# Rope scores as two float32r matmuls over stacked halves, and forgetting attention transposed by key block

## Chip, cores, metric

The kernel runs on one core of one Trainium2 chip. The metric is device time in microseconds (us) of one launch, less is better. Times are medians of a few executions; one further execution was taken with the hardware profiler, and all rows come from it.

## What is computed

Three transformer blocks follow one another on one sequence of 512 tokens with 1024 features, all in float32: block 1 (mLSTM beside differential attention, a feed-forward, a gated embedding), block 2 (a stick-breaking attention layer, then a latent attention layer) and block 3 (feed-forward, a hybrid of a spatial gating unit and a "forgetting" attention, feed-forward). Two pieces matter here.

Latent attention, 8 heads: each query and key has 128 "nope" features of its own and 64 "rope" features that are rotated by position; the rope key is shared by all heads before its norm.

```
k = concatenate([k_nope, k_pe], axis=-1)          # 128 + 64 features
q = rms_norm(q, q_head_norm); k = rms_norm(k, k_head_norm)
q = concatenate([q[..., :128], rope(q[..., 128:], pos)], axis=-1)
k = concatenate([k[..., :128], rope(k[..., 128:], pos)], axis=-1)
o = causal_softmax_attention(q, k, v, 1 / sqrt(192))
```

Forgetting attention, 8 heads of 64 features, in blocks of 128 queries:

```
logits = q_block @ k[:q1].T * scale + cum[q] - cum[k]    # cum: running sum of log forget gates
p = softmax(where(kpos <= qpos, logits, -1e30))
out_block = p @ v[:q1]
```

## The kernel before

Features lie on partitions and tokens on the free axis, so a tile is 128 features by 512 tokens. The large products with weights are made in three float32r matmuls for each 128 input features: weights and activations are split into a high part (rounded to float32r by a ScalarE copy) and a low part (VectorE subtracts the high part), and hi·hi, lo·hi and hi·lo are summed in PSUM (lines 429 to 431 for feature-major outputs, 439 to 441 for token-major ones; tiles `hi`, `lo`, `wh`, `wl`, output `pm`). The matmuls of attention take float32 operands as they are. In the rows a float32 matmul is two instructions, a float32r or bfloat16 one is one.

**Order.** The Python code is a program order; a list scheduler then places each instruction on its engine, and every engine runs its own list in order. The attention loops hide the latency of softmax in two ways: `self.fill()` takes the next piece from a list of projections that are not urgent, and `self.later(f, depth)` puts transposes and values of a finished block of queries into a queue, whose pieces are run some steps later. `flush()` empties that queue at the end and takes one filler after each piece.

**Latent attention** (`mla`) goes by 4 pairs of heads. For a pair, `kv`, `q`, `scales` and `keys` make its operands; for pairs 1 to 3 they are fillers in the loop of the pair before. `keys` broadcasts the 16 per-token key scales over partitions by matmuls with an identity: once for the shared rope key (line 1287, tile `pbc`, 8 matmuls of 64 output rows, product `krc` on line 1289), and once for each head's nope key (line 1292, tile `bc`). A score block is three matmuls into one PSUM bank (tile `mls`): the nope part over 128 rows (line 1326), the rope part over 64 rows, the upper or lower half of the partitions by head (line 1327), and the causal mask as bfloat16 (line 1328). Blocks are 128 queries by 512, 384, 256 and 128 keys.

**Forgetting attention** (`fox_pair`) also goes by 4 pairs of heads and 4 query blocks from the longest to the shortest. Scores (`fxs`, lines 1712 and 1714) of the two heads go to two PSUM banks of the role `sc`; softmax leaves a tile `fxp` for each head. One step later `apply` transposes the block's key blocks (line 947, tile `tr`, one PSUM bank of the role `tr` that both heads use in turn; ScalarE copies it to `aT` on line 949) and multiplies by the values (line 1701, tile `fxo`, 64 output rows for each head). The spatial gating unit is a filler here: its last projections run in the loop of pair 3, its norm's statistic and the first half of the output projection (`out_a`) behind them.

## Time and profile before

| | before |
|---|---|
| median of 3 executions | 2506.77 us (2504.44 to 2509.23) |
| the profiled execution | 2498.9 us |
| its span, first to last instruction | 2497.1 us |
| TensorE (PE) busy | 2438.4 us, 98% |
| VectorE (DVE), ScalarE (ACT), GpSimd (POOL) busy | 53%, 39%, 3% |
| mean granted TensorE clock | 0.988 of full speed |
| HBM traffic | 96 GB/s over the span |

A matmul's record runs from its start to its modelled end, and the next one starts before that end, so in a stream of matmuls the cost of one is the distance to the next start. The busy time of a group counts overlapped time once.

### The profile page before, as it was taken

The numbers are of one execution on the slowest core, as the hardware profiler recorded it, in microseconds if no ns is written. First come the engines' busy times: TensorE is split into PE (matmuls) and PEld (weight loads), VectorE is DVE, ScalarE is ACT, GpSimd is POOL, SyncE is SP. The second block draws the span as 40 slices with busy tenths as digits, with TensorE's granted clock in tenths as the row PEclk, the third lists the DMA queues.
The fourth block names the chain that finished last, engine by engine and source line by source line (L and its number), as shares of the span: only waits on it lengthen the run. The fifth ranks groups of instructions, "written<-read, shape, count | busy, mean of one in ns | idle before, by whom it ended". The sixth has DMA issues, their size and how long they took to land. (4 is left out here: it accounts for less than half of the span.)

```text
span 2497.1 us, 31348 instructions
## 1 busy us (share of the span) xinstructions
PE 2438.4 (98%) x12622; PEld 1994.1 (80%) x12622; DVE 1313.5 (53%) x2220; ACT 983.0 (39%) x1575; POOL 62.7 (3%) x62
## 2 busy tenths in 40 slices
PE   8999999999999999999999999999999999999998
PEld 6877788888888787777877798888898768888887
DVE  7536556774775664446555654223365465432333
ACT  5423433442444445655324533222245344322221
POOL 0000000000000000000000000000010001000001
PEclk9999999999999999999999999999999989999999
DMA  5223225433433332222322113233213101323321
GB/s 188 93 90 101 90 97 185 135 123 114 152 119 119 126 109 77 68 81 83 113 71 85 37 66 118 93 101 101 93 54 103 61 26 60 96 93 101 100 87 49
DMA packets 71746, 240.78 MB, mean 96 GB/s; under 512 B 8232, under 2 KB 11184, under 8 KB 71600
## 3 DMA queue, kind: packets, MB, share of 16 engines
q1 hardware_dynamic: 71600, 238.78, 29.1%
q8 instruction: 99, 1.62, 0.3%
q14 instruction: 47, 0.39, 0.0%
HBM read 236.64 MB, written 2.11 MB: 96 GB/s over the span
## 5 line engine op out<-in xcount | busy, mean ns | idle before, releaser
L429 PE MATMUL pm<-hi,wh 128*128 128x512 f32 (+1 forms) x2736 | 1045.1, 383 | 11.1 <-ACT hi L393 7.3
L430 PE MATMUL pm<-lo,wh 128*128 128x512 f32 (+1 forms) x2736 | 1042.8, 381 | 0.0
L431 PE MATMUL pm<-hi,wl 128*128 128x512 f32 (+1 forms) x2736 | 1040.7, 380 | 0.0
L419 ACT CAST wh<-raw 128x1024 fp32r<-128x1024 f32 (+1 forms) x372 | 382.3, 1029 | 827.0 <-PE pm L430 581.5
L420 DVE TENSOR_TENSOR wl<-raw,wh 128x1024 fp32r<-128x1024 f32 (+1 forms) x372 | 445.0, 1196 | 448.8 <-ACT wh L419 422.2
L429 PEld LDWEIGHTS pm<-hi,wh 128*128 128x128 f32 x2736 | 517.2, 189 | 110.9 <-ACT hi L393 8.9
L430 PEld LDWEIGHTS pm<-lo,wh 128*128 128x128 f32 x2736 | 517.0, 189 | 96.5 <-issue 3.8
L431 PEld LDWEIGHTS pm<-hi,wl 128*128 128x128 f32 x2736 | 516.8, 189 | 96.1 <-issue 3.6
L439 PE MATMUL pm<-wh,hi 128*128 128x256 f32 x400 | 116.0, 290 | 4.9 <-ACT vt L816 4.9
L1393 DVE CUSTOM_DVE_ANT_0 adaw<-adaw,cb 128x1024 f32<-128x1024 f32 x72 | 87.9, 1220 | 55.7 <-DMA adaw<-in_w_ada 55.5
L441 PE MATMUL pm<-wh,lo 128*128 128x256 f32 x400 | 115.1, 288 | 0.0
L440 PE MATMUL pm<-wl,hi 128*128 128x256 f32 x400 | 114.2, 286 | 0.0
L1472 DVE TENSOR_TENSOR sg<-sg,pm 128x512 f32<-128x512 f32 x44 | 30.2, 686 | 132.8 <-PE pm L431 132.7
L572 POOL TENSOR_TENSOR rc<-ms,nhalf 128x4 f32<-128x4 f32 (+2 forms) x29 | 38.6, 1333 | 2335.2 <-DVE ms L577 1779.3
L439 PEld LDWEIGHTS pm<-wh,hi 128*128 128x128 f32 x400 | 77.8, 194 | 5.8 <-ACT vt L816 5.3
L441 PEld LDWEIGHTS pm<-wh,lo 128*128 128x128 f32 x400 | 77.8, 194 | 0.5 <-issue 0.3
L440 PEld LDWEIGHTS pm<-wl,hi 128*128 128x128 f32 x400 | 77.8, 194 | 0.5 <-issue 0.2
L481 PE MATMUL pm<-hi,wh 128*128 128x256 f32 (+1 forms) x216 | 61.5, 309 | 9.9 <-ACT hi L400 7.1
L970 DVE SCALAR_TENSOR_TENSOR uy<-ur,vec,uy 128x511 f32<-128x511 f32 x88 | 65.7, 747 | 9.0 <-ACT uy L968 8.0
L258 DVE TENSOR_TENSOR acc<-acc,sq 128x512 f32<-128x512 f32 (+1 forms) x93 | 54.6, 595 | 24.0 <-ACT sq L254 22.8
L482 PE MATMUL pm<-lo,wh 128*128 128x256 f32 (+1 forms) x216 | 66.0, 307 | 0.3 <-DVE lo L1424 0.3
L483 PE MATMUL pm<-hi,wl 128*128 128x256 f32 (+1 forms) x216 | 66.2, 308 | 0.0
(350 smaller groups left out, 2363.7 us busy)
## 6 DMA issues: line engine op xcount, KB each, us to landing
raw<-in_w_gu SPq DMA_DIRECT2D x88, 512.0 KB, 3.3
adaw<-in_w_ada SPq DMA_DIRECT2D x72, 512.0 KB, 3.3
raw<-in_w_dn SPq DMA_DIRECT2D x48, 512.0 KB, 3.3
raw<-in_w_up SPq DMA_DIRECT2D x44, 512.0 KB, 3.3
raw<-in_w_g SPq DMA_DIRECT2D x16, 512.0 KB, 3.3
raw<-in_w_l0qk SPq DMA_DIRECT2D x16, 512.0 KB, 3.4
raw<-in_w_l SPq DMA_DIRECT2D x12, 512.0 KB, 3.3
X<-in_x SPq DMA_DIRECT2D x16, 256.0 KB, 5.6
```

The costliest lines, as they stand in the source:

```text
L419: nc.scalar.copy(wh[:, :n], raw[:, :n])
L420: nc.vector.tensor_tensor(wl[:, :n], raw[:, :n], wh[:, :n].bitcast(F32), ALU.subtract)
L429: self.nc.tensor.matmul(out, a, xh, start=start and k == 0, stop=False)
L430: self.nc.tensor.matmul(out, a, xl, start=False, stop=False)
L431: self.pe = self.nc.tensor.matmul(out, b, xh, start=False, stop=stop and k == n - 1)
L439: self.nc.tensor.matmul(out, xh[:, sl], a, start=start and k == 0, stop=False)
L440: self.nc.tensor.matmul(out, xh[:, sl], b, start=False, stop=False)
L441: self.pe = self.nc.tensor.matmul(out, xl[:, sl], a, start=False, stop=stop and k == len(x) - 1)
L482: self.nc.tensor.matmul(o[:, sl], wh[:, k], xl[:, sl], start=False, stop=False)
L483: self.nc.tensor.matmul(o[:, sl], wl[:, k], xh[:, sl], start=False, stop=k == 7)
L970: nc.vector.scalar_tensor_tensor(y[:, sh:], raw[:, :S - sh], self.v("fconv_w", 44 * (2 - sh) + f), y[:, sh:], mult, add)
L1393: nc.vector.tensor_tensor_reduce(w, w, cb, 0.5, 0.0, ALU.mult, ALU.add, mod[:, i:i + 1])
```

## The change

In latent attention the rope query of each head becomes one tile `qs` of 128 rows: its high part in 64 rows and its low part in the other 64. The rope key is scaled for each head apart (the same broadcast `bc` that scales the nope key), and split into two float32r tiles of 128 rows (both halves hold the shared key), kept in buffers of the weight pools (`krs`). Scores then take two float32r matmuls over 128 rows, with the key's high and its low part. The eight `pbc` matmuls of a pair are gone.

In forgetting attention the probabilities of a pair of heads stay in five tiles until all four query blocks are done. Then, in the next pair's loop, they are transposed by key block: five groups of four blocks, each filling one PSUM bank, in banks of the roles `tr` and `ms` in turn, and a last piece `values` multiplies each key block once by all its queries (512, 384, 256 and 128 columns).

```diff
-                r["qr"] = self.rope(r["q"].pop(0), self.v("qh_r"), cos, sin)
+                qr = self.rope(r["q"].pop(0), self.v("qh_r"), cos, sin)
+                r["qr"] = []
+                for own, other in (ROWS, ROWS[::-1]):
+                    y = self.t(F32R, "qs")
+                    nc.scalar.copy(y[own], qr[own])
+                    nc.vector.tensor_tensor(y[other], qr[own], y[own].bitcast(F32), ALU.subtract)
+                    r["qr"].append(y)
...
             def keys():
                 rs = r["rs"]
-                bk = self.psa("pbc")
-                for j in range(NB):
-                    for par in range(2):
-                        nc.tensor.matmul(bk[64 * par:64 * par + 64, j * P:(j + 1) * P], rs[:, 4 * j + par:4 * j + par + 1].to_broadcast([P, 64]), self.ident, start=True, stop=True)
-                r["kr"] = self.t(F32, "krc")
-                nc.vector.tensor_tensor(r["kr"], kr, bk, mult)
+                r["kr"] = []
                 for par in range(2):
                     b = self.bcast_ps([rs[:, 4 * j + par:4 * j + par + 1] for j in range(NB)])
                     nc.vector.scalar_tensor_tensor(r["k"][par], r["k"][par], gqk, b, mult, mult)
+                    y = self.q(F32, "krc")
+                    nc.vector.tensor_tensor(y, kr, b, mult)
+                    w = (self.whp, self.wlp)[par].tile([P, 1024], F32R, tag=("wh", "wl")[par], name="krs")
+                    h, l = w[:, 0:S], w[:, S:2 * S]
+                    nc.scalar.copy(h, y)
+                    nc.vector.tensor_tensor(l, y, h.bitcast(F32), ALU.subtract)
+                    r["kr"].append((h, l))
...
-                    nc.tensor.matmul(ps[:, :n], cur["qr"][rp, qb * P:n], cur["kr"][rp, :n], start=False, stop=False)
+                    for kr_part in cur["kr"][par]:
+                        nc.tensor.matmul(ps[:, :n], cur["qr"][par][:, qb * P:n], kr_part[:, :n], start=False, stop=False)
...
     def fox_pair(self, q, k, vt, c, cl, cum, out, norm):
+        both = self.t(F32, "fxp")
+        tiles = [[self.t(F32, "fxp") for _ in range(2)] for _ in ROWS]
+        prob = [{3: t[0], 2: t[1][:, 0:3 * P], 0: t[1][:, 3 * P:], 1: both[:, 2 * P * par:2 * P * par + 2 * P]} for par, t in enumerate(tiles)]
+        aT = [{}, {}]
+        def turned(role, blocks):
+            ps, y, o = self.psa("tr", role), self.t(F32, "aT"), 0
+            for par, kb in blocks:
+                aT[par][kb] = y[:, o:o + S - kb * P]
+                for qb in range(kb, NB):
+                    nc.tensor.transpose(ps[:, o:o + P], prob[par][qb][:, kb * P:(kb + 1) * P], self.ident)
+                    o += P
+            nc.scalar.copy(y, ps)
+        def values():
+            po = self.psa("fxo", "po")
+            for kb in range(NB):
                 for par, r in enumerate(ROWS):
                     col = (kb % 2) * 256 + (2 * cl + par) * 64
-                    nc.tensor.matmul(po[0][r, qb * P:P * (qb + 1)], vt[kb // 2][:, col:col + 64], aT[par][:, kb * P:(kb + 1) * P], start=kb == 0, stop=kb == qb)
+                    nc.tensor.matmul(po[r, kb * P:], vt[kb // 2][:, col:col + 64], aT[par][kb], start=kb == 0, stop=kb == NB - 1, skip_group_check=True)
...
             self.fill()
-            self.later(lambda p=prob, qb=qb: apply(p, qb), 1)
+            self.step()
+        self.queue += [
+            lambda: turn2([(0, 0)], [(1, 0)]),
+            lambda: turn2([(0, 1), (0, 3)], [(1, 1), (1, 3)]),
+            lambda: turn2([(0, 2), (1, 2)]),
+            values,
+        ]
```

On PE, the first score blocks of latent attention stood so before (`mls` is the score bank, `bc` the broadcast of key scales, `pm` a projection):

```order
L584 MATMUL bc<-cst,rc 128x128 x4
L441 MATMUL pm<-wh,lo 128x256
L584 MATMUL bc<-cst,rc 128x128 x4
L1326 MATMUL mls<-kn,qn 128x512
L1327 MATMUL mls<-krc,ropeo 128x512
L1328 LDWEIGHTS bf_ident
L1328 MATMUL mls<-bf_mask_q,bf_ident 128x128
L1326 MATMUL mls<-kn,qn 128x384
```

Now, at the same place:

```order
L584 MATMUL bc<-cst,rc 128x128 x4
L1335 MATMUL mls<-kn,qn 128x512
L584 MATMUL bc<-cst,rc 128x128 x4
L1337 MATMUL mls<-krs,qs 128x512 x2
L1338 LDWEIGHTS bf_ident
L1338 MATMUL mls<-bf_mask_q,bf_ident 128x128
L429 MATMUL pm<-hi,wh 128x512
L430 MATMUL pm<-lo,wh 128x512
```

The first nope score moved ahead of the second broadcast, two float32r instructions stand where one float32 matmul stood, and projections of the next pair that stood ahead of these rows now stand behind them.

On PE, in pair 1 of forgetting attention, the last apply of pair 0 (one transpose `tr` and one values matmul `fxo` for each head) stood so before, inside a stream of projections:

```order
L429 MATMUL pm<-hi,wh 128x512
L947 MATMUL tr<-cst,fxp 128x128
L1701 MATMUL fxo<-aT,fvt 64x128
L430 MATMUL pm<-lo,wh 128x512
L1701 MATMUL fxo<-aT,fvt 64x128
L431 MATMUL pm<-hi,wl 128x512
```

Now all values of pair 0 stand together, at the end of pair 1's loop and ahead of pair 2's first scores (`fxs`):

```order
L441 MATMUL pm<-wh,lo 128x256
L1725 MATMUL fxo<-aT,fvt 64x512 x2
L1725 MATMUL fxo<-aT,fvt 64x384 x2
L1725 MATMUL fxo<-aT,fvt 64x256 x2
L1725 MATMUL fxo<-aT,fvt 64x128 x2
L1735 MATMUL fxs<-fqk 128x512 x2
```

The four separate applies of a pair became one group of eight matmuls, one pair later. From the first score to the last value of forgetting attention, the stretches of other matmuls that interrupt the float32r ones go from 32 to 21 in PE's list.

On PE, the end of forgetting attention, from the gating unit's statistic (`bc` broadcasts its reciprocal root) to the first `out_a` matmuls (line 429), stood so before:

```order
L584 MATMUL bc<-cst,rc 128x128
L947 MATMUL tr<-cst,fxp 128x128 x3
L1701 MATMUL fxo<-aT,fvt 64x128
L584 MATMUL bc<-cst,rc 128x128 x2
L1701 MATMUL fxo<-aT,fvt 64x128 x5
L584 MATMUL bc<-cst,rc 128x128
L947 MATMUL tr<-cst,fxp 128x128 x2
L429 MATMUL pm<-hi,wh 128x512 x4
```

Now, from the last values of pair 2 on:

```order
L1725 MATMUL fxo<-aT,fvt 64x128 x2
L560 MATMUL colsum<-ones,acc 128x1 x4
L584 MATMUL bc<-cst,rc 128x128 x4
L1716 MATMUL tr<-cst,fxp 128x128 x8
L429 MATMUL pm<-hi,wh 128x512 x3
```

All transposes of pair 3 (eight here, then eight and four between the `out_a` matmuls) and its values now come behind the last scores, where only the last two query blocks' were left.

## Rows read from the trace of the kernel before

**Rows 1.** The page's busy times of the engines (share of the span, instructions).

```profile
PE 2438.4 (98%) x12622; PEld 1994.1 (80%) x12622; DVE 1313.5 (53%) x2220; ACT 983.0 (39%) x1575; POOL 62.7 (3%) x62
```

**Rows 2.** By stretch: length, busy PE, PEld, DVE, ACT, POOL; PEclk, DMA, GB/s.

```profile
1262.00:1416.00 154.00, 150.83 (x859) 111.19 (x858) 93.03 (x229) 59.86 (x137) 11.60 (x4) 0.98 0.20 65
1899.90:2026.00 126.10, 125.69 (x809) 95.09 (x808) 72.69 (x211) 57.62 (x121) 2.30 (x4) 1.00 0.21 70
2026.00:2068.30 42.30, 34.64 (x181) 25.80 (x180) 21.05 (x53) 15.74 (x33) 2.17 (x2) 0.80 0.10 32
```

**Rows 3.** PE's timeline, latent attention's scores: start, length, line, operands, instructions.

```profile
1274.13 1.02 PE L1326 MATMUL mls<-kn,qn 128*128 128x512 f32 x2
1275.08 1.12 PE L1327 MATMUL mls<-krc,ropeo 64*128 64x512 f32 x2
1276.14 0.23 PE L1328 MATMUL mls<-bf_mask_q,bf_ident 128*128 128x128 bf16 x1
...
1279.06 0.70 PE L1327 MATMUL mls<-krc,ropeo 64*128 64x256 f32 x2
1279.69 0.23 PE L1328 MATMUL mls<-bf_mask_q,bf_ident 128*128 128x128 bf16 x1
...
1288.98 0.48 PE L1327 MATMUL mls<-krc,ropeo 64*128 64x128 f32 x2
1289.40 0.23 PE L1328 MATMUL mls<-bf_mask_q,bf_ident 128*128 128x128 bf16 x1
```

**Rows 4.** PE's timeline, mLSTM: float32r matmuls (line 831) ahead of a bfloat16 mask.

```profile
113.74 0.33 PE L831 MATMUL pd<-R,pick 128*128 128x128 f32 x1
113.91 0.23 PE L832 MATMUL pd<-bf_mask_t,bf_ident 128*128 128x128 bf16 x1
...
126.39 0.40 PE L831 MATMUL pd<-R,pick 128*128 128x512 f32 x1
126.63 0.23 PE L832 MATMUL pd<-bf_mask_t,bf_ident 128*128 128x128 bf16 x1
```

**Rows 5.** PE's timeline: float32r matmuls behind float32 broadcasts over the full array.

```profile
2064.76 0.36 PE L429 MATMUL pm<-hi,wh 128*128 128x256 f32 x1
2064.97 0.28 PE L430 MATMUL pm<-lo,wh 128*128 128x256 f32 x1
2065.08 0.29 PE L431 MATMUL pm<-hi,wl 128*128 128x256 f32 x1
```

**Rows 6.** Busy time by stretch, line 1287 alone (`pbc`): length, PE, PEld.

```profile
1262.00:1416.00 154.00, 4.38 (x64) 3.41 (x64) 0.98 0.20 65
```

**Rows 7.** Groups of latent attention's stretch: line, form, count, busy, mean ns, idle before.

```profile
L1289 DVE TENSOR_TENSOR krc<-ropeo,pbc 128x512 f32<-128x512 f32 x4 | 2.7, 676 | 0.5 <-PE pbc L1287 0.5
L419 ACT CAST wh<-raw 128x512 fp32r<-128x512 f32 x1 | 0.6, 618 | 1.4 <-PE pm L441 1.4
```

**Rows 8.** Busy time by stretch, line 1701 (`fxo`, the values) alone.

```profile
1899.90:2026.00 126.10, 14.44 (x120) 8.61 (x120) 1.00 0.21 70
2026.00:2068.30 42.30, 6.36 (x40) 3.96 (x40) 0.80 0.10 32
```

**Rows 9.** The same for line 1186, the values of block 2's stick-breaking attention, 8 pairs.

```profile
900.00:1180.00 280.00, 29.40 (x128) 10.52 (x128) 0.99 0.25 81
```

**Rows 10.** The same for line 947 (`tr`), forgetting attention.

```profile
1899.90:2026.00 126.10, 11.26 (x60) 6.88 (x60) 1.00 0.21 70
```

**Rows 11.** PE's timeline at the end of forgetting attention; in brackets idle time and releaser.

```profile
2027.05 0.66 PE L947 MATMUL tr<-cst,fxp 128*128 128x128 f32 x4
2027.64 0.70 PE L1712 MATMUL fxs<-fqk 64*128 64x256 f32 x4
...
2031.77 1.11 PE L947 MATMUL tr<-cst,fxp 128*128 128x128 f32 x4 [3.21 <-ACT aT L949]
```

**Rows 12.** Busy time by stretch where the clock was at half.

```profile
1320.40:1327.20 6.80, 6.80 (x26) 6.10 (x25) 3.51 (x8) 2.58 (x5) 0.00 (x0) 0.50 0.22 77
2030.40:2044.00 13.60, 11.64 (x52) 8.64 (x54) 5.29 (x23) 5.72 (x15) 1.16 (x1) 0.50 0.04 15
```

More of the change, by code (lines that the diff above doesn't have):

```diff
@@ L1321, in mla @@
             for par in range(2):
-                rp = slice(64 * par, 64 * par + 64)
                 for qb in range(NB - 1, -1, -1):
@@ L1691, in fox_pair @@
         mult, add = ALU.mult, ALU.add
-        po = []
-        def apply(ps, qb):
-            if not po:
-                po.append(self.psa("fxo", "po"))
-            aT = [self.transposed(p, qb) for p in ps]
-            for kb in range(qb + 1):
+        both = self.t(F32, "fxp")
[13 more added lines that the diff above has]
+            for kb in range(NB):
                 for par, r in enumerate(ROWS):
                     col = (kb % 2) * 256 + (2 * cl + par) * 64
-                    nc.tensor.matmul(po[0][r, qb * P:P * (qb + 1)], vt[kb // 2][:, col:col + 64], aT[par][:, kb * P:(kb + 1) * P], start=kb == 0, stop=kb == qb)
-            if qb == 0:
-                y = self.t(F32, "fxo")
-                nc.vector.tensor_copy(y, po[0])
-                out.append(y)
-                norm.add(c, y)
+                    nc.tensor.matmul(po[r, kb * P:], vt[kb // 2][:, col:col + 64], aT[par][kb], start=kb == 0, stop=kb == NB - 1, skip_group_check=True)
+            y = self.t(F32, "fxo")
+            nc.vector.tensor_copy(y, po)
+            out.append(y)
+            norm.add(c, y)
         for qb in range(NB - 1, -1, -1):
@@ L1714, in fox_pair, with turn2 @@
                 nc.tensor.matmul(ps[:, qb * P:n], self.bf["ident"], self.bf["mask_q"], start=False, stop=True)
-            prob = []
             for par, ps in enumerate(sc):
                 cb = cum[2 * c + par]
-                p = self.t(F32, "fxp")
+                p = prob[par][qb]
                 mx = self.s(4, "mx")
-                nc.vector.tensor_tensor_reduce(p[:, :n], ps[:, :n], cb[:, :n], 1.0, 4 * NEG, add, ALU.max, mx[:, 0:1])
+                nc.vector.tensor_tensor_reduce(p, ps[:, :n], cb[:, :n], 1.0, 4 * NEG, add, ALU.max, mx[:, 0:1])
                 nc.vector.tensor_scalar(mx[:, 1:2], mx[:, 0:1], -1.0, None, mult)
-                self.last = nc.scalar.activation(p[:, :n], p[:, :n], AF.Exp, bias=mx[:, 1:2], scale=1.0, accum_out=mx[:, 2:3])
+                self.last = nc.scalar.activation(p, p, AF.Exp, bias=mx[:, 1:2], scale=1.0, accum_out=mx[:, 2:3])
                 nc.vector.reciprocal(mx[:, 3:4], mx[:, 2:3])
-                nc.vector.tensor_scalar(p[:, :n], p[:, :n], mx[:, 3:4], None, mult)
-                prob.append(p)
+                nc.vector.tensor_scalar(p, p, mx[:, 3:4], None, mult)
             self.fill()
-            self.later(lambda p=prob, qb=qb: apply(p, qb), 1)
+            self.step()
+        def turn2(*what):
+            for role, blocks in zip(("tr", "ms"), what):
+                turned(role, blocks)
+        self.queue += [
[4 more added lines that the diff above has]
+        ]
     def block3(self, x, out):
```

## The prediction

> **What bounds the kernel now.** I read the page first: PE is busy 98% of the span, DVE 53%, ACT 39% [rows 1], so a microsecond taken from PE's list is a microsecond of the span wherever PE isn't waiting. The second view is busy time by stretch. In latent attention's scores (1262 to 1416 us) PE is busy 150.8 of 154.0 us, DVE 93.0 and ACT 59.9; in the larger part of forgetting attention (1899.9 to 2026) PE is busy 125.7 of 126.1; only its end (2026 to 2068.3) is different, with PE busy 34.6 of 42.3 us at a mean clock of 0.80 [rows 2]. So the change works on 280 us in which PE is the bound, and on 42 us in which chains of small DVE and ACT steps are. The third view is PE's timeline, where the distance between starts is the price of an instruction. Beside 2.4 GHz there are stretches at half of it, 1.2 GHz [rows 12]: the longest, 13.6 us, begins after PE stood idle for 3.21 us, waiting for ACT's copy of a transpose [rows 11].
>
> **The change part by part: latent attention.** One rope matmul over 64 rows costs 1.06 us at 512 keys (1275.08 to 1276.14), 0.63 at 256 and 0.42 at 128 [rows 3]; for 384 I take the middle of its neighbours, 0.84. That is 2.95 us for a head, 23.6 us for eight.
>
> Two float32r matmuls take its place. The second stands ahead of the mask, as line 831 does: 0.24 us at 512, 0.17 at 128 [rows 4]. At 256 a float32r matmul in a stream costs 0.11 to 0.12 (2064.97 to 2065.08), so 384 gets the middle, 0.18. The first stands behind a float32 matmul, and there the row shows more: 0.21 at 256 just behind float32 broadcasts, 0.09 more than the next one [rows 5]. Without this surcharge the new pairs cost 2 x (0.24 + 0.18 + 0.12 + 0.17) = 1.42 us a head, with it on each first one 1.78: 11.4 to 14.2 us for eight heads. The nearest row has the surcharge, so I take 14.2: a saving of **9.4** (9.4 to 12.2).
>
> The Trainium skill ("TensorEngine Tiling (Array Packing)", section Key Properties) says that changing the tiling mode drains TensorE. By it alone, going from float32 to float32r on the full array would be free, and the 0.09 us by which the nope score's second half is dearer where the 64-row mode follows would go too, on 32 matmuls: 12.2 + 2.9 = 15.1 us instead of 9.4. The trace agrees for the mode (a 64-row matmul of 512 costs 1.06 us, a 128-row one 0.95 to its successor [rows 3]), but shows the same surcharge without a change of mode [rows 5], so I stay with 9.4.
>
> The `pbc` broadcasts go: 4.4 us of PE [rows 6], nothing instead, since both products now read the broadcast that is there anyway. Saving **4.4**.
>
> Added off PE, for each pair: one `krc` product more, two casts and two subtractions for the keys, two casts and two subtractions on 64 rows for the queries. With 0.68 us for a DVE pass of 512 and 0.62 for a cast [rows 7] (half the rows bring at most the same price) that is 5 x 0.68 = 3.4 us DVE and 4 x 0.62 = 2.5 us ACT a pair, 13.6 and 9.9 in all: DVE goes from 93.0 to 107 us in a stretch of about 141, so it stays below PE. What covers it for pairs 1 to 3 is the loop of the pair before, in which `keys` is a filler. For pair 0 little does: in the new order broadcast, nope score, second broadcast and rope matmuls stand next to each other, and the rope needs k's scaling, `krc`, cast and subtraction, 0.68 + 0.68 + 0.62 + 0.68 = 2.7 us, against 0.95 us of nope score and a broadcast. The projections that stood ahead are still done later, so this idle is a true loss: about **2** us (0 to 2.7), once. If the other pairs lose their cover it is 2 us each.
>
> Latent attention: 9.4 + 4.4 - 2 = **12 us** (8 to 17; the bottom with 2 us of idle more at two of the other pairs, the top 12.2 + 4.4 without any idle).
>
> **Forgetting attention.** The values of three pairs took 14.44 us while the clock was full, 4.8 a pair [rows 8]. The new form (64 output rows, 512, 384, 256 and 128 columns, two heads) stands in the trace already: stick-breaking's line 1186 has the same shapes, 29.40 us for 8 pairs, 3.7 a pair [rows 9]. Saving 1.1 x 4 = **4.5**. Transposes: 60 took 11.26 us, 0.188 each [rows 10]; four in one block take 0.59 from their first start to the next instruction (2027.05 to 2027.64), 0.147 each [rows 11]. All but none now come in blocks of four or eight: 80 x 0.04 = **3.3**. Streams of float32r are interrupted 21 times where it was 32, and each return to them costs 0.09 [rows 5]: **1**. ACT copies five tiles of 512 for a pair instead of eight of mixed width, DVE is unchanged; both have room [rows 2].
>
> The end of this stage has three waits and the half clock. Pair 3's values took 6.36 us there [rows 8], 1.5 more than at full clock. The chain that sets the pace (last projection, gelu steps, statistic, `gn_a`, splits) is untouched, but PE has fewer small things queued ahead of its `colsum`; against that, all five groups of pair 3 now come behind the last scores, each waiting for ACT's copy of the one before on its bank. I take a gain of **2** (-5 to +8: all of the second half of that half-clock stretch back, or a second one like it).
>
> Forgetting attention: 4.5 + 3.3 + 1 + 2 = **11 us** (4 to 17).
>
> **Sum.** 12 + 11 = 23 us: the profiled execution would go from 2498.9 to 2476. It lies 7.9 us under the median of the runs, 2506.8; on that scale the forecast is **2484 us**.
>
> **The rivals.**
> *Only the rope part comes through* (0.17). The end of forgetting attention waits for its chain, and with pair 3's transposes and values moved behind it gives back what pairs 0 to 2 saved. For it: 7.7 us without PE work in 42.3 [rows 2], and the new order of the tail. Against: three of the four pairs lie before 2026, where PE hardly waits. Gain 8 to 16, with latent attention's 12 alone 2495.
> *The clock stays full in the tail* (0.13). The idle of 3.21 us came because both heads shared the one bank `tr` [rows 11]; with `tr` and `ms` in turn the second block needn't wait for the first copy. If that idle goes, the half-clock stretch may go: its 11.64 us of PE work [rows 12] would take 5.8, so 3.2 + 5.8 = 9 more on top of 23, and with the cheap float32r entries 36: 2471.
> *Slower: PE waits at the start of each pair* (0.05). The chain broadcast, scaling, `krc`, cast, subtraction through the single bank `ms` takes some 3.2 us with the broadcast. If nothing else stands there at all four pairs, PE idles 3.2 us, and half clock follows as it did behind the idle of 3.21 [rows 11]; a half-clock stretch of 6.8 us [rows 12] does what 3.4 would do. 4 x 6.6 = 26 us against 23: 2510. It decides only if the wait is nearly the whole chain at all four pairs; the order has fillers there for three.
> *Float32r over 128 rows is as slow as float32* would turn the rope part into a loss. One record for each of line 831's matmuls, 0.24 us at 512, where float32 takes two and 0.95, excludes it [rows 3, 4].
>
> **How the numbers follow.** The likeliest case, a gain of 16 to 30 us, has 0.55: 2477 to 2491 on the scale of the medians. Rivals as above; 0.10 is left for gains under 8 us without one cause, half of it within 0.2% (5 us, about what a measurement of this kernel can tell from no change). Faster: 0.55 + 0.17 + 0.13 + 0.05 = 0.90; same 0.05; slower 0.05. The range reaches 13 us up into the rope-only case and 16 down into the full-clock one: 2468 to 2497.
>
> **What would show it.** The two new float32r lines of the scores should cost some 14 us by their starts in place of 23.6, with line 1287 gone; PE's waits in latent attention should list a new one on DVE's `krs` of 1 to 3 us at pair 0 and little else. The values should fall from 20.8 us to about 15, the transposes to 12 or 13. The stretch up to the last gating projection should be 8 to 12 us shorter, the tail about as long, with one half-clock stretch near its start. I am wrong if the first float32r matmul behind a float32 one costs over 0.5 us, if every pair waits for `krs`, or if the tail's half clock lasts much longer than 17 us.

## The result and the profile after

The changed kernel takes 2477.48 us (median of 4 executions, 2473.0 to 2482.2) against 2505.61 us of the kernel before on the same chip: ratio 0.9888, 95% interval 0.9860 to 0.9917, or 28 us less. A second comparison, with five rounds, gave 0.9906 (0.9891 to 0.9922), 23.5 us. The profiled execution took 2473.0 us, its span is 2471.1 us.

The page's first part, busy time of the engines, answers to [rows 1]:

```profile
PE 2406.2 (97%) x12462; PEld 1980.4 (80%) x12462; DVE 1324.0 (54%) x2240; ACT 991.8 (40%) x1579; POOL 64.2 (3%) x62
```

PE lost 32.2 us of busy time and the span 26.0: some 6 us of what was saved came back as idle time. Where, two marks per stage tell, both starts of records. From latent attention's first `swap<-lat` (1243.62 us before, 1243.43 after) to its last `mlo` (1422.00 and 1412.49) it took 178.4 us and takes 169.1. Between the stages nothing moved (477.9 us both times). From the first `fxs` (1899.91 and 1890.38) to the last `fxo` (2056.72 and 2032.25) it took 156.8 us and takes 141.9. So latent attention gave 9.3 us and forgetting attention 14.9; another 2.0 us came right behind the last `fxo`: from it to the `pm` records that wait for `gn_b`'s split it is 11.6 us before and 9.6 after.

Busy time by stretch, columns as in [rows 2]: latent attention, forgetting attention to the last gating projection, its tail, and two stretches in which the granted clock was at half, 1.2 GHz:

```profile
1243.40:1412.50 169.10, 158.76 (x925) 128.19 (x924) 112.64 (x262) 76.06 (x166) 11.60 (x4) 0.97 0.18 56
1890.40:2002.30 111.90, 111.21 (x709) 86.81 (x708) 71.92 (x215) 56.04 (x112) 3.10 (x4) 1.00 0.24 78
2002.30:2041.90 39.60, 33.45 (x186) 24.03 (x185) 20.95 (x48) 16.28 (x31) 2.86 (x2) 0.91 0.13 40
...
1329.70:1333.10 3.40, 2.96 (x14) 2.96 (x14) 0.81 (x2) 1.84 (x4) 0.39 (x1) 0.50 0.00 0
...
2015.80:2022.60 6.80, 5.71 (x18) 4.84 (x19) 6.32 (x14) 3.76 (x7) 0.00 (x0) 0.50 0.00 0
```

Latent attention now has 10.3 us in 169.1 without PE work, where PE stood without work for 3.2 us of 154 [rows 2]. The tail's clock is 0.91 where it was 0.80: one half-clock stretch of 6.8 us stands there in place of one of 13.6 and one of 3.4.

PE's timeline at the first score block, which answers to [rows 3]:

```profile
1271.43 0.71 PE L1337 MATMUL mls<-krs,qs 128*128 128x512 f32 x2
1271.99 0.23 PE L1338 MATMUL mls<-bf_mask_q,bf_ident 128*128 128x128 bf16 x1
...
1276.35 0.59 PE L1337 MATMUL mls<-krs,qs 128*128 128x256 f32 x2
1276.78 0.23 PE L1338 MATMUL mls<-bf_mask_q,bf_ident 128*128 128x128 bf16 x1
```

The two float32r instructions cost 0.56 us at 512 keys (1271.43 to 1271.99) and 0.43 at 256, where one float32 matmul cost 1.06 and 0.63. Added up by starts over all 64 records, the rope part fell from 23.9 to 13.3 us. The `pbc` matmuls, 4.1 us by starts, are gone.

PE's waits in latent attention (us in total, times, longest):

```profile
PE bc L584 <- POOL rc L572: 6.4, 3, 2.1
PE mls L1335 <- ACT p L1344: 1.8, 4, 0.6
PE mls L1335 <- DVE kn L1294: 0.8, 1, 0.8
PE swap L1379 <- DVE ms L1285: 0.6, 3, 0.3
```

The first line is a wait for GpSimd's power of the 16 scales, once at each of pairs 1 to 3. The kernel before had a smaller one: there `pbc` was the first broadcast behind the power, and the same list for its latent attention begins

```profile
PE pbc L1287 <- POOL rc L572: 1.7, 2, 1.4
```

The timeline at pair 2 now, first PE, then POOL:

```profile
1326.89 1.12 PE L1379 MATMUL swap<-qn,cst 128*128 128x512 f32 x2 [0.19 <-DVE ms L1285]
1330.14 2.08 PE L584 MATMUL bc<-cst,rc 128*128 128x128 f32 x8 [2.13 <-POOL rc L572]
1332.01 0.64 PE L1314 MATMUL mlo<-aT,mv 128*128 128x128 f32 x2
...
1334.00 1.12 PE L1335 MATMUL mls<-kn,qn 128*128 128x512 f32 x2 [0.64 <-ACT p L1344]
```

```profile
1327.19 2.90 POOL L572 TENSOR_TENSOR rc<-ms,nhalf 128x16 f32<-128x16 f32 x1 [36.16 <-DVE ms L1286]
```

The power takes 2.90 us and starts while `swap` runs; the next thing in PE's list behind `swap` is `bc`, which needs it. All projections of the next pair are done by then. PE idles 2.13 us, and the 8 `bc` records then take 1.87 us by starts, where eight of them took 0.81 at full clock (1270.62 to 1271.43): the clock has gone to half. At pair 1 the stretch of 3.4 us begins at 1292.1, at pair 3 at 1370.6.

The transposes of forgetting attention (line, form, count, busy, mean ns, idle before), which answer to [rows 10], and the busy time of line 1725 alone, the values, which answers to [rows 8]:

```profile
L1716 PE MATMUL tr<-cst,fxp 128*128 128x128 f32 x80 | 12.8, 294 | 1.8 <-DVE fxp L1746 1.8
...
1890.40:2041.90 151.50, 12.29 (x64) 4.25 (x64) 0.98 0.21 68
```

The values are busy 12.3 us (20.8 before: 14.44 + 6.36), 11.6 by starts (18.5 before). Transposes cost 10.8 us by starts (15.3 before, of which 2.0 are the wait of a projection that came next). The waits of the stage and of what comes right behind it:

```profile
PE bc L584 <- POOL rc L572: 3.1, 2, 1.7
PE tr L1716 <- DVE fxp L1746: 1.8, 1, 1.8
PE pm L429 <- ACT hi L393: 1.3, 1, 1.3
PE fxs L1735 <- DVE mx L1742: 0.6, 1, 0.6
```

The 3.21 us on ACT's `aT` [rows 11] are gone; in their place the tail has 1.4 us on the gating norm's power and 1.8 on the last softmax.

### The profile page after: what moved, and what is told of

Its sections match the earlier page's. It is cut to its first block, busy times and chain, and to the rows that moved or that the text cites. A ratio compares the mean times of both kernels' runs of the same rounds, so it can differ in the third digit from the quotient of the medians.

```text
span 2471.1 us, 31023 instructions
## 1 busy us (share of the span) xinstructions
PE 2406.2 (97%) x12462; PEld 1980.4 (80%) x12462; DVE 1324.0 (54%) x2240; ACT 991.8 (40%) x1579; POOL 64.2 (3%) x62
```

## The experiments

The theory after the first look at this profile: both halves of the change take the PE work away that they should, and latent attention gives part of it back to the three waits for GpSimd's power and to the half clock behind them. The rivals: the loss is the longer chain to the split rope key; or the float32r scores are worth less than their starts say.

In the table, "latent" runs from the first `swap<-lat` to the last `mlo` and "forgetting" from the first `fxs` to the last `fxo`, in us of the profiled execution; "half" is how much of it the granted clock was at half. Each kernel has one profiled execution. The runs were made in sets, and each ratio is to the kernel before as it ran in the same set: 2505.6 us in the first comparison, 2499.2 for the two halves, key scales and gates, 2501.1 for the second comparison, both edits, float32 rope and values by query block, 2498.5 for the other four.

| kernel | us | ratio to before (interval) | latent, half | forgetting, half |
|---|---|---|---|---|
| before | 2505.6 | 1 | 178.4, 6.8 | 156.8, 17.0 |
| changed | 2477.5 | 0.9888 (0.9860 to 0.9917) | 169.1, 10.2 | 141.9, 6.8 |
| changed, second comparison | 2477.7 | 0.9906 (0.9891 to 0.9922) | 171.6, 23.9 | 141.8, 6.8 |
| latent half alone | 2492.3 | 0.9972 (0.9960 to 0.9984) | 168.0, 10.2 | 157.0, 17.1 |
| forgetting half alone | 2483.2 | 0.9948 (0.9930 to 0.9967) | 175.2, 0 | 141.4, 6.8 |
| key scales early | 2477.0 | 0.9920 (0.9906 to 0.9934) | 169.6, 13.7 | 141.6, 6.8 |
| gate ahead of keys | 2467.8 | 0.9879 (0.9865 to 0.9894) | 163.5, 0 | 140.4, 3.4 |
| both edits of order | 2469.5 | 0.9869 (0.9853 to 0.9885) | 163.7, 0 | 145.2, 13.6 |
| float32 rope | 2478.8 | 0.9910 (0.9895 to 0.9924) | 173.1, 0 | 141.7, 6.8 |
| float32 rope, gate ahead | 2486.0 | 0.9940 (0.9922 to 0.9959) | 182.9, 13.7 | 141.9, 6.8 |
| float32 rope, full array | 2485.7 | 0.9949 (0.9933 to 0.9966) | 180.6, 20.5 | 141.4, 6.8 |
| values by query block | 2476.3 | 0.9897 (0.9881 to 0.9913) | 171.9, 23.9 | 137.8, 0 |
| values in three places | 2478.0 | 0.9914 (0.9897 to 0.9931) | 170.1, 13.7 | 142.3, 6.8 |
| one bank for transposes | 2478.8 | 0.9918 (0.9902 to 0.9935) | 171.3, 20.5 | 143.8, 6.8 |

**The halves apart.** One kernel has `mla` of after and `fox_pair` of before, the other the reverse.

> The latent attention half of the change alone; forgetting attention as before. First theory (the two halves don't touch each other; latent attention loses part of its gain to three waits for GpSimd's power of the key scales): 9 us under the kernel before (7 to 12), with the same three waits of bc on rc of about 2.1 us, 6.4 in all, each with a half-clock stretch behind it. Rival (the later stage depends on the earlier one, by buffers or by what the clock has left): clearly more or less than 9 us, so that this run and that of the other half don't add up to 26 us of the two profiles.

> The forgetting attention half of the change alone; latent attention as before. First theory: 17 us under the kernel before (14 to 20), of which about 14 before the last gating projection and 3 behind it, values at about 11.6 us by their starts in place of 18.5, and no half-clock stretch of 13.6 us in the tail. Rival (the halves depend on each other): the two halves together don't make 26 us.

7 us for the latent half (4 to 10), at the lower edge of what was expected, and 13 us for the forgetting half (8 to 17), below its 14 to 20. Its six executions spread from 2480.3 to 2491.9 us, and the profile is of the fastest. In the profiles the stages moved by 10.3 and 15.5 us, the waits of `bc` on `rc` are 6.4 us at three places again, and the values cost 11.6 us by starts again. Added up, the medians make 20 us, not the 26 that the theory expected; 20 is at the edge of what the whole change gave (28, and 23.5 in the second comparison).

> The changed kernel once more, beside the others of this set. If the two halves don't touch each other, its ratio to the kernel before is the product of those of the halves alone, 0.9972 x 0.9948 = 0.992 (20 us). If they help each other, it stays at the 0.9888 of the first comparison (28 us).

0.9906 lies between the two answers and its interval leaves out the 0.9888, but holds 0.992; the first interval holds 0.9906. So nothing here shows that the halves help each other. The second profile of the same kernel shows where its executions differ: 23.9 us at half clock in latent attention in place of 10.2, and the stage 2.5 us longer.

**The wait for the power.** The first of two edits takes the key's scales in a power of their own, right behind `kv`:

```diff
                     r["k"].append(y)
+                r["ks"] = scaled(slice(0, 2))
...
+            def scaled(cols):
+                m, s = self.s(16, "ms"), self.s(16, "rc")
+                at = lambda t: t[:, 0:16].rearrange("p (j c) -> p j c", c=4)[:, :, cols]
+                nc.vector.tensor_tensor(at(m), at(r["sums"]), at(mulc), mult)
+                nc.vector.tensor_tensor(at(m), at(m), at(addc), add)
+                nc.gpsimd.tensor_tensor(at(s), at(m), at(self.nhalf), ALU.pow)
+                return s
+
             def scales():
-                m = self.s(16, "ms")
-                nc.vector.tensor_tensor(m, r["sums"][:, 0:16], mulc, mult)
-                nc.vector.tensor_tensor(m, m, addc, add)
-                r["rs"] = self.rpow(m, 16)
+                r["rs"] = scaled(slice(2, 4))
...
-                rs = r["rs"]
+                rs = r["ks"]
```

> The changed kernel, with the key scales' power taken right behind kv (8 columns) and the query scales' right behind q (8 columns), in place of one power of 16 columns behind both; TensorE's order stays the same. First theory (latent attention loses to the wait for GpSimd's power): the three waits of bc on rc, 6.4 us, fall under 1 us, the half-clock stretches behind them go (3 x 3.4 us, which do what 1.7 us each would do), and the time falls 6 to 11 us under the changed kernel, 34 to 39 us under the kernel before. Rival (the loss is the longer chain of scaling, product, cast and subtraction to the rope operands): the wait moves from bc to the first mls of each pair on krs or kn, 1 to 3 us each, and the time stays within 2 us of the changed kernel.

The wait fell from 6.4 to 2.8 us, but the stage didn't get shorter (169.6 us): `mls<-p` rose from 1.8 to 2.8 us, `mlo<-aT` from 0.3 to 2.3, half clock from 10.2 to 13.7. Both theories miss: the time is within 2 us of the changed kernel, as the rival has it, but no wait for `krs` appears. The timeline at pair 2 shows what is next in line (PE, POOL and DVE together):

```profile
1328.00 1.12 PE L1385 MATMUL swap<-qn,cst 128*128 128x512 f32 x2 [0.18 <-DVE ms L1287]
1328.32 1.64 POOL L1289 TENSOR_TENSOR rc<-ms,nhalf 128x8 f32<-128x8 f32 x1 [7.37 <-DVE ms L1288]
1329.23 0.69 DVE L1387 TENSOR_TENSOR ropea<-swap,sin 128x512 f32<-128x512 f32 x1 [0.64 <-PE swap L1385]
...
1330.07 1.13 PE L584 MATMUL bc<-cst,rc 128*128 128x128 f32 x8 [0.94 <-POOL rc L1289]
```

The power shown here is the query's; `bc` in this kernel reads only the key's, which was done 9 us before. But `swap` and `bc` share the single PSUM bank of the role `ms`, and `ropea`, which reads `swap`, ends at 1329.92; `bc` starts 0.15 us later, and likewise at the two other pairs (0.15 and 0.14). The view puts the wait down to POOL because the two ends lie 0.04 us apart. Behind it PE comes to scores whose softmax isn't ready. So the power was the last of several things that are all late at this place; what is missing is work for PE while they run.

The second edit supplies that work: one of the gate projections (24 float32r matmuls), which stood behind `keys` at pairs 0 and 1 and in the last pair's loop, stands ahead of it at each of pairs 1 to 3.

```diff
-                self.fillers += work
-            self.fillers += [gates[3:4], gates[4:5], [], [idle] * 4 + [gates[5]] + [idle] * 3 + gates[6:]][c]
+                self.fillers += work[:3] + [gates[3 + c]] + work[3:]
+            if c == 3:
+                self.fillers += [idle] * 8 + gates[6:]
```

> The changed kernel, with one gate projection (24 float32r matmuls, some 5.6 us) put between scales and keys of each of pairs 1 to 3, in place of behind them. First theory: it covers GpSimd's power, the waits of bc on rc fall under 1 us, and the time falls 6 to 11 us under the changed kernel, less by up to 4 us if the gate projections are then missing where they stood. Rival (chain to krs, or too little work at the end of each pair's loop whatever its order): the wait reappears behind the gate or at the next pair, within 2 us of the changed kernel.

Latent attention's stretch and its waits:

```profile
1246.46:1409.94 163.48, 157.54 (x936) 127.03 (x935) 116.14 (x268) 78.44 (x170) 11.60 (x4) 1.00 0.20 67
```

```profile
PE mls L1336 <- ACT p L1345: 2.7, 4, 1.5
PE pm L431 <- DVE wl L420: 1.3, 2, 0.7
PE mls L1336 <- DVE kn L1294: 0.8, 1, 0.8
PE mlo L1314 <- ACT aT L949: 0.6, 3, 0.2
```

No wait on `rc` is left, the clock is full throughout, and the stage takes 163.5 us, 5.6 and 8.1 less than in the changed kernel's two profiles, although 12 more projection matmuls stand in it (302 `pm` records in place of 290). In the same set it ran 9 us under the kernel with early scales, whose time is the changed kernel's; the changed kernel itself didn't run in that set, and by the ratios the gain over it is 7 us on the second comparison and 2 on the first. The theory of missing cover holds, and the kernel with both edits, below, ran 8 us under the changed one in the same set.

**What float32r is worth.** The rope scores go back to one float32 matmul over 64 rows, with the key scaled by each head's own broadcast, so `pbc` stays away:

```diff
-                    for kr_part in cur["kr"][par]:
-                        nc.tensor.matmul(ps[:, :n], cur["qr"][par][:, qb * P:n], kr_part[:, :n], start=False, stop=False)
+                    nc.tensor.matmul(ps[:, :n], cur["qr"][ROWS[par], qb * P:n], cur["kr"][par][:, :n], start=False, stop=False)
```

> The changed kernel with the rope scores back as one float32 matmul over 64 rows; the key is still scaled by each head's own broadcast, so the eight pbc matmuls of a pair stay away, and the splits of key and query go. First theory (the two float32r matmuls save what the distance of starts says, 23.9 against 13.3 us): 8 to 11 us slower than the changed kernel. Rival (what float32r saves is lost again in waits for the longer chain and in half clock): within 3 us of the changed kernel, with the waits of bc on rc shorter.

The rival comes close: 2478.8 against 2477.7 us of the changed kernel in the same set. Its latent attention and its largest wait there:

```profile
1244.09:1417.22 173.13, 170.15 (x929) 126.04 (x928) 107.03 (x250) 69.37 (x154) 11.60 (x4) 1.00 0.20 64
```

```profile
PE bc L584 <- POOL rc L572: 1.1, 3, 0.4
```

Here the rope part costs 23.5 us by starts, 10.2 more than in the changed kernel, yet the stage is only 1.5 to 4.1 us longer than in the changed kernel's two profiles. PE's list explains it: here a score and the values of an earlier block stand between `swap` and `bc` (1.9 us of work by their starts), so the power is nearly covered, idle time is 3.0 us where it was 10.3, and the clock never falls. In the changed kernel `bc` stands right behind `swap`, and the score behind it. So the 10 us were saved, and mostly given back at the three pairs' ends.

The cross-check takes float32 rope together with the gate projections ahead of `keys` (both diffs above):

> The float32 rope scores over 64 rows (as in the run with float32 rope) together with one gate projection between scales and keys of pairs 1 to 3. First theory (float32r does save some 10 us of TensorE's time, and the changed kernel loses it to waits for GpSimd's power and to half clock, which the gate projections prevent): with float32 there is little to cover, so the gate is worth 0 to 3 us here, against 8 in the changed kernel, and this kernel is 8 to 11 us slower than the changed one with the same gates. Rival (the place of the gate projections is worth 6 to 8 us whatever the rope scores are, and float32r is worth nothing): 6 to 9 us under the run with float32 rope, within 3 us of the changed kernel with gates.

The gates bring nothing here; they cost some 7 us (0.9910 to 0.9940, in different sets). The six executions spread from 2478.1 to 2488.1 us, and the profile is of one at 2487.2; the two fastest, 2478.1 and 2480.6, are at the time of float32 rope without gates and have the highest mean clocks of the six (0.991 and 0.989, the others 0.986 to 0.987). So what the gates bring in the changed kernel isn't the worth of the place as such, and with them in place float32r is worth 15 us by the ratios (0.9879 against 0.9940) and 19.4 by the stage, more than forecast. Some 9 us of it are the rope part itself (23.5 and 14.2 us by starts), and by the fastest executions the two kernels are 11 us apart; the rest goes with half clock, 13.7 us of it in this stage against none. What made the clock fall here stays open: PE's busy share is higher (178.5 of 182.9 us) than with float32r and gates, where it stayed full.

**Rows or precision.** The float32 rope matmul over all 128 rows, the other half of the query zero:

```diff
+                r["qr"] = []
+                for own, other in (ROWS, ROWS[::-1]):
+                    y = self.t(F32, "qs")
+                    nc.scalar.copy(y[own], qr[own])
+                    nc.vector.memset(y[other], 0.0)
+                    r["qr"].append(y)
```

> The rope scores as one float32 matmul over all 128 rows: the query's own half, the other 64 rows zero, against the key scaled for the head. The same sums as over 64 rows, so only the rows that the array uses differ from the run with float32 rope. If the rows cost nothing, rope matmuls cost what the nope ones do, 0.87 us at 512 in place of 1.05, some 3 us less over 32 of them, and the nope ones ahead lose their surcharge of 0.09 us too: 3 to 6 us under the run with float32 rope. Rival (the surcharge belongs to the matmul that follows, whatever its rows): the same time within 2 us. The Trainium skill (TensorEngine Tiling (Array Packing), section Key Properties) says that a change of the tiling mode drains TensorE; by it the first answer is the right one.

By starts the first answer is right, and more so than expected. The timeline at the first block:

```profile
1277.31 1.02 PE L1330 MATMUL mls<-krs,qs 128*128 128x512 f32 x2
1278.17 0.22 PE L1331 MATMUL mls<-bf_mask_q,bf_ident 128*128 128x128 bf16 x1
```

0.86 us at 512 against 1.05 over 64 rows in the kernel with float32 rope; over all 32 matmuls 17.0 against 23.5 us, about 0.2 us for each whatever its columns. And yet this kernel is 7 us slower than that one by the medians and by the stage, which neither answer has (its profiled execution is the longest of six, 7 us over their median): its list has `bc` right behind `swap` again, and its waits are the changed kernel's:

```profile
PE bc L584 <- POOL rc L572: 6.4, 3, 2.2
PE mls L1329 <- ACT p L1337: 2.1, 5, 0.7
PE swap L1372 <- DVE ms L1284: 1.1, 3, 0.6
```

With 6.5 us less of rope work the kernel is slower, its idle time is up from 3.0 to 11.8 us, and 20.5 us are at half clock. This is the same trade as in the changed kernel, without float32r.

**The values.** Two kernels separate the width of the values matmuls from their place. The first has 20 matmuls of 128 columns a pair, all in one piece:

```diff
-            for kb in range(NB):
+            for qb, kb in [(qb, kb) for qb in range(NB - 1, -1, -1) for kb in range(qb + 1)]:
...
-                    nc.tensor.matmul(po[r, kb * P:], vt[kb // 2][:, col:col + 64], aT[par][kb], start=kb == 0, stop=kb == NB - 1, skip_group_check=True)
+                    nc.tensor.matmul(po[r, qb * P:P * (qb + 1)], vt[kb // 2][:, col:col + 64], aT[par][kb][:, (qb - kb) * P:(qb - kb + 1) * P], start=kb == 0, stop=kb == qb)
```

> The changed kernel with the same transposes by key block, but the values of a pair as 20 matmuls of 128 columns again, all in one place, in place of eight of 512 to 128. If the values' saving (18.5 to 11.6 us by their starts) comes of the wide matmuls, they go back to some 18 us and the kernel is 5 to 8 us slower than the changed one. If it comes of standing together, without transposes and projections between, they stay at 11 to 13 us and the time within 2 us.

By starts they come to 13.9 us, of which 3.1 us are waits of other instructions right behind them: 10.8 us without these. The time is the changed kernel's within the intervals, and in this profile forgetting attention is even 4 us shorter, with the clock full throughout. Width brings nothing. The second spreads the wide matmuls over three pieces of the queue:

```diff
-            lambda: turn2([(0, 1), (0, 3)], [(1, 1), (1, 3)]),
-            lambda: turn2([(0, 2), (1, 2)]),
-            values,
+            lambda: (turn2([(0, 1), (0, 3)], [(1, 1), (1, 3)]), values(0)),
+            lambda: (turn2([(0, 2), (1, 2)]), values(1)),
+            lambda: values(2, 3),
```

> The changed kernel with the values of a pair in three places (key block 0, then 1, then 2 and 3, each with the transposes of that step) in place of one. If the values are cheaper because they stand together (11.6 us by their starts, 18.5 before): 13 to 16 us by their starts and the kernel 2 to 4 us slower than the changed one. Rival (any form in which the two heads' matmuls follow each other in pairs is as cheap): 11 to 12.5 us by their starts and the time within 1.5 us.

12.0 us by starts and the same time within the intervals: gathering them from these places into one brings at most 0.4 us. What is left is that the two heads' matmuls follow each other. The changed kernel's own timeline shows it, since the scheduler has torn one pair's values apart. Key block 0 at 512 columns, both heads together (x4, two instructions each) and one head alone (x2), each with its successor:

```profile
1980.37 1.08 PE L1725 MATMUL fxo<-aT,fvt 128*64 128x512 f32 x4
1981.38 0.50 PE L429 MATMUL pm<-hi,wh 128*128 128x512 f32 x1
...
2004.78 1.07 PE L1725 MATMUL fxo<-aT,fvt 128*64 128x512 f32 x2
2005.78 0.66 PE L1716 MATMUL tr<-cst,fxp 128*128 128x128 f32 x4
```

Two heads take 1.01 us and one head takes 1.00. The second head's record starts 0.006 to 0.007 us behind the first's: the two halves of 64 output columns run at the same time, and a matmul that stands alone leaves the other half empty. The Trainium skill says so of tiles ("TensorEngine Tiling (Array Packing)", section Key Properties: different tiles can execute their loads and matmuls in parallel); the trace agrees.

Before, 20 of the 80 values matmuls stood alone in PE's list. One of them in the kernel before, with its successor, and two heads side by side in the kernel with values by query block:

```profile
1951.02 0.43 PE L1701 MATMUL fxo<-aT,fvt 128*64 128x128 f32 x2
1951.38 0.50 PE L431 MATMUL pm<-hi,wl 128*128 128x512 f32 x1
...
1985.62 0.44 PE L1725 MATMUL fxo<-aT,fvt 128*64 128x128 f32 x4
1985.99 0.50 PE L429 MATMUL pm<-hi,wh 128*128 128x512 f32 x1
```

One takes 0.36 us and two take 0.37. So the pairs explain some half of the 6.9 us by starts: 19 of the 20 stood at full clock and took 6.8 us, and as pairs would take 3.5, an estimate from these rows. Another 2.1 us are the clock, since 4.3 us of the values' starts lay at half clock before and none does now. The rest, some 1.5 us, has no run of its own; it goes with fewer separate places in PE's list, 10 in place of 32.

**Two banks or the order.** All transposes through one bank:

```diff
-            for role, blocks in zip(("tr", "ms"), what):
+            for role, blocks in zip(("tr", "tr"), what):
```

> The changed kernel with all transposes of forgetting attention through the one bank tr, in place of tr and ms in turn. If the two banks are what took the 3.2 us of idle and most of the half clock out of the end of forgetting attention: a new wait of tr on ACT's aT of 2 to 3 us in the tail, a half-clock stretch of 10 us or more, 4 to 9 us slower than the changed kernel. Rival (the order does it: now projections stand between the groups of transposes, so a group needn't wait for the copy of the one before): within 2 us of the changed kernel.

The wait on ACT's copy is there, in the stage's list:

```profile
PE tr L1716 <- ACT aT L1718: 2.3, 3, 1.6
```

But it is 2.3 us at three places, the stage has 6.8 us at half clock as in the changed kernel, and is 2.0 us longer; the times are within each other's intervals (0.9918 and 0.9906). So the second bank is worth some 2 us at most, and not the half clock. What made the wait of 3.21 us before [rows 11] so long stands in ACT's list:

```profile
2030.62 0.63 ACT L1502 ACTIVATE ge<-ge 128x512 f32<-128x512 f32 x1 [1.97 <-DVE ge L1501]
2031.15 0.57 ACT L949 COPY aT<-tr 128x512 f32<-128x512 f32 x1
```

The transposes were through at 2027.64, but the copy stood behind a step of the gating unit's gelu that waited for VectorE, and so came 3.5 us later. In the kernel with one bank the copy is late for the same reason (2016.15, behind transposes that were through at 2013.23), but PE has more work to do meanwhile, and the wait is 1.6 us. The short half clock then comes with the order, in which projections stand between the groups of transposes; that is argued, since no run here has two banks and the old order.

**Both edits of order.** The gate projections ahead of `keys`, and pair 3's transposes from the short key blocks to the long one, so that the first group needs only two query blocks:

```diff
-            lambda: turn2([(0, 0)], [(1, 0)]),
-            lambda: turn2([(0, 1), (0, 3)], [(1, 1), (1, 3)]),
-            lambda: turn2([(0, 2), (1, 2)]),
+            lambda: turn2([(0, 2), (1, 2)]),
+            lambda: turn2([(0, 1), (0, 3)], [(1, 1), (1, 3)]),
+            lambda: turn2([(0, 0)], [(1, 0)]),
```

> The changed kernel with two edits of order: one gate projection between scales and keys of pairs 1 to 3 of latent attention, and the transposes of forgetting attention from the short key blocks to the long one, so that pair 3's first group needs only its first two query blocks. First theory (the changed kernel loses to places where TensorE has nothing ready, the waits for GpSimd's power at pairs 1 to 3 and the 3.2 us of waits behind the gating unit's statistic): 5 to 8 us from the first, 2 to 4 from the second, 7 to 12 us under the changed kernel, and no half-clock stretch in latent attention. Rival (work drawn forward leaves a hole of the same size further on): within 2 us of the changed kernel, with new waits for p, aT or hi of the same sum.

8.2 us under the changed kernel in the same set, so it beats both kernels. All of it is the first edit's: latent attention takes 163.7 us without half clock, as it did with that edit alone. In the tail the rival was right: six transposes stand in front of the gating norm's broadcast, and its wait falls from 1.4 us, put down to the power, to 0.8, put down to ACT's copy of a transpose; but a new wait of 2.4 us stands 9 us earlier (`tr`, put down to DVE's gating tile `gt`), a half-clock stretch of 13.7 us begins behind it, and forgetting attention is 4.8 us longer than with the first edit alone. The two kernels' intervals overlap.

## Why the prediction was right

The forecast was 2484 us and 23 us of gain; measured were 2477.5 and 28, and 23.5 in the second comparison. The total held. That it came so near is in part luck, since its two halves were off in opposite ways.

**Right, in mechanism and size.** PE is the bound, and most of the PE work went as worked out. The rope part: 14.2 us forecast, 13.3 by starts. The broadcasts: 4.4 forecast, 4.1. Transposes: "12 or 13", 12.8 busy. The first half-clock stretch of the tail is there, near its start.

**Mis-sized: idle in latent attention.** The step was "about 2 us (0 to 2.7), once", at pair 0 for the chain to `krs`, with "what covers it for pairs 1 to 3 is the loop of the pair before". At pair 0 the wait is 0.8 us, and it is for `kn`. At pairs 1 to 3 the cover failed: by the time `scales` and `keys` come, PE has done all of the loop's projections, since the scheduler draws them forward. Waits rose from 3.1 to 9.9 us, and half clock from 6.8 to 10.2 us (23.9 in the other profile). That cost about as much as float32r brought: with float32 rope scores and the rest of the change the time is 1 us longer, a difference that the intervals don't tell from none. Of the 14.7 us of rope and broadcasts that went by starts, the stage kept 9.3 in one profile and 6.8 in the other: a loss of 5 to 8 us, where 2 were forecast. The kernel with gates, which has the cover, shows what the change can bring there: 14.9 us, where rope and broadcasts went down by 13.8.

The rival "PE waits at the start of each pair" had the place nearly right (three of four pairs, some 2 us each, half clock behind each), but not the chain: it named scaling, `krc`, cast and subtraction, where the runs show the power on GpSimd, then the bank `ms`, then the softmax. It couldn't decide the sign, since it cost less than 10 us and not 26.

**Mis-sized: forgetting attention.** Forecast 4.5 + 3.3 + 1 + 2 = 11 us, measured 14.9 to the last value and 16.9 with the 2.0 behind it. Split by estimates from the rows, the 14.9 are: 4.7 for half clock (PE did 15.0 us of work at half before, 11.64 of them in the long stretch [rows 12], and 5.7 now; a stretch at half does half the work), 2.2 for waits (6.0 to 3.8), some 5 for the values (6.9 by starts without the 2.1 of clock), some 2 for the transposes, and 1 left over, which no run takes apart (the interruptions were forecast at 1). So the term that was too small is the tail: 2 us forecast, nearly 7 measured, within its own range (-5 to +8). That is much of the rival *the clock stays full in the tail*, and the reason it gave, two banks, isn't the cause: with one bank the stage has 6.8 us at half as well.

The values' term, 4.5, is near what the starts gave, but not for its reason: they were to be busy "about 15" us, the price of [rows 9], and are busy 12.3, with 2.1 of the fall due to the clock. What sets the price is not the shape but whether the other head's matmul runs beside it; in line 1186's trace 44 of the 128 records have none beside them, here 12 of 64.

**The rule weighed.** The prediction weighed what the Trainium skill says ("TensorEngine Tiling (Array Packing)", section Key Properties), that a change of the tiling mode drains TensorE. Its rows put the price at 0.09 us on a neighbouring matmul; the kernel over the full array shows 0.2 us on each 64-row matmul itself, 6.5 us of the 10.6 that the rope part lost. So most of that part's saving is the 128 rows, and the smaller part float32r. The surcharge on the first float32r matmul behind a float32 one, which kept the forecast at 14.2, is also seen, and at this block is larger than its 0.09: at 256 keys 0.43 us for two (1276.35 to 1276.78), against 0.12 each in a stream [rows 5].

## What to carry to other kernels

When an engine is 98% busy, work taken from it shows in full only where something else is ready to run; read the places where a chain of small steps on the other engines (here a 2.9 us power on GpSimd, one shared PSUM bank, a softmax) was hidden by exactly that work, and move other work there in the same change. Put matmuls that use half of the array's columns next to the one that uses the other half; their width matters little. Check a stage by its own length and its granted clock, since a total can come out as forecast while two terms are wrong.

## What was not expected of the hardware

- A float32 matmul over 64 rows between full-array ones costs some 0.2 us more than the same over 128 rows (1.05 and 0.86 us at 512, 23.5 and 17.0 us over 32), whatever its columns.
- Two 64-column float32 matmuls on the two halves of the columns take the time of one (1.01 and 1.00 us at 512).
- Idle time and half clock don't follow one from the other simply: behind each idle of 2.1 us at a pair's end the clock fell for 3.4 us or more; in the kernel with gates it stayed full through waits of up to 1.5 us; with float32 rope and gates it fell at 1320.5 us, where the only wait of the 8 us before was 0.6. What decides it is left open.
